# A ten-phase network on one core: the S5 tables are prepared beside another stage, the modulation's matrix is read in three parts

## The chip, the cores and the metric

The kernel runs on one core of a Trainium2 chip. The metric is device time in microseconds, the median of runs. The engines are TensorE (PE, with its weight loads as PEld), VectorE (DVE), ScalarE (ACT), GpSimd (POOL) and SyncE (SP), which only issues transfers here. P is 128, T is 512.

## The reference

Two blocks run one behind the other on an activation of 512 tokens by 1024 channels, all in float32. The first block has a gated delta-net mixer, a convolutional feed-forward network (FFN), a chunked attention and a second FFN. The second block has two layers; each is modulated by six vectors of 1024 that come from the condition `c` by a matrix.

```python
cond = jax.nn.silu(c)
for i in range(DEPTH):
    mod = cond @ ada_w[i] + ada_b[i]                    # 1024 x 6144, for each layer
    sh1, sc1, g1, sh2, sc2, g2 = jnp.split(mod[:, None, :], N_MOD, axis=-1)
    h = _modulate(_rmsnorm(x, norm_mix_g[i]), sh1, sc1)
    y = _s5_mixer(h, ...) if i % 2 == 0 else _ssd_mixer(h, ...)
    x = x + g1 * y
    h = _modulate(_rmsnorm(x, norm_mlp_g[i]), sh2, sc2)
    x = x + g2 * _sq_relu_mlp(h, mlp_w1[i], mlp_w2[i])
```

The S5 mixer is a linear recurrence for 64 groups of 64 complex states. Powers of its transition, and its input and output matrices multiplied by them, depend on parameters alone; the kernel prepares them as tables before the mixer begins.

## The kernel before, in words

The phases run in the order gdn, ffn0, attn, ffn1, s5, mlp0, ssd, mlp1, and a final norm. The activation stays in SBUF as eight tiles `h` of 128 channels by 512 tokens. Every weight matrix is read in chunks of 128 by 1024 float32 (512 KB) in one fixed order, `queue`. `next()` hands out a chunk: ScalarE rounds it to a high part (L305), VectorE subtracts to get the low part (L306), and TensorE takes three matmuls for each pair of parts (L347 to L349), 24 matmuls of 512 columns a chunk. Raw, high and low parts have three buffers each, and the read of a chunk is issued three chunks ahead, from SP's queue.

An FFN has 44 up chunks and 24 down chunks, in the order 20 up, 8 down, 16 up, 8 down, 8 up, 8 down. Behind an up chunk VectorE scales the result (L598), and takes two of three taps of a convolution (L607); once in a pair of chunks it multiplies gate and value (L978) and splits the product (L566). Behind a down chunk it adds to `h` (L577). The MLPs have 32 chunks in and 32 out. Their first four chunks are taken by the stage before as heads.

Work that no phase needs at once runs in the background. `bg` is a list of Python generators, and each call of `next()` advances the first of them by `bgrate` steps. So the background's instructions stand in the program between weight chunks; a scheduler of the framework then orders each engine's instructions by program order and by its own account of when each is ready, and each engine keeps that order on the chip. There are three kinds of background:

- `ada_bg` reads the modulation's matrix in 96 chunks of 512 KB (two buffers, `araw`), multiplies each by its part of the condition and adds it up on VectorE (L1142), in three thirds; each third ends with small matmuls. All three run beside ffn0.
- `shift_bg` sums a shift vector through the head weights of a phase (`s5_in`, the MLPs', the SSD's), 128 columns at a time on VectorE (L1402). The sums for s5 and mlp0 run beside ffn1, those for ssd and mlp1 beside mlp0.
- `s5_prep_bg` prepares the S5 tables beside ffn1, behind the shift sums. Its first five steps compute exponentials, sines and quotients for all groups on VectorE. Then each of eight tiles has five steps: `angles` (VectorE with two sines on ScalarE, on the tiles `exm` and `scm`), `taps` and `b_out` of the tile before, `c_pow` and `b_pow`. The last two are twelve GpSimd instructions of 512 columns a tile and a few small ones. `taps` multiplies their result on TensorE into a bank of PSUM and VectorE writes it to `ks` (L1330), from where eight transfers take it to DRAM; `b_out` transposes `BL` on TensorE (L1356) into two banks. The background's lane has two banks of PSUM, so the second transpose goes to the bank that `taps` used and waits until `ks` has been read from it.

Work tiles of the preparation have one buffer each. `s5_tables` reads the finished tables of a tile back from DRAM, four transfers of 1.8 MB together; the first two tiles' reads are issued with the end of `s5_prep_bg`, the others in the S5 phase.

Of the kernel before, what the change touches and what calls it, by code (L numbers as in the profile page):

```python
# [20 lines left out]
P = 128  # L21
# [199 lines left out]
def r3(ap, n):  # L221
    return ap.rearrange("p (a b) -> p a b", a=n)


class Net:
    def __init__(self, ctx, tc, aps, pcols, out):
# [21 lines left out]
        self.rcol = self.cpool.tile([P, 4], F32, name="rcol")  # L248
# [708 lines left out]
    def ffn(self, l):  # L957
        nc = self.nc
        v, s = nc.vector, nc.scalar
        with ExitStack() as es:  # L960
# [6 lines left out]
            for name, c in self.ffn_seq(l):  # L967
                self.bgrate = 2 if l == 0 and ("down" in name or c >= 36) else 1
# [159 lines left out]
    def ada_bg(self):  # L1128

        nc = self.nc  # L1130
        v = nc.vector
        cond = self.cond
        nc.scalar.activation(cond, self.p("cond"), AF.Silu)
        for q in range(3):
            acc = self.apool.tile([P, 1024], F32, tag="acc", name=self.nm("acc"), bufs=1)
            for k in range(32):
                raw = self.apool.tile([P, 1024], F32, tag="araw", name=self.nm("araw"), bufs=2)
                nc.sync.dma_start(out=raw, in_=self.aps["ada"][q, k])
                if k == 0:
                    v.tensor_scalar(out=acc, in0=raw, scalar1=cond[:, 0:1], scalar2=None, op0=ALU.mult)  # L1140
                else:
                    v.scalar_tensor_tensor(out=acc, in0=raw, scalar=cond[:, k:k + 1], in1=acc,  # L1142
                                           op0=ALU.mult, op1=ALU.add)
                yield
            yield
            ps = self.bank("bg")
            for k in range(8):
                nc.tensor.matmul(ps[:, 4 * k:4 * k + 4], acc[:, k * P:(k + 1) * P], self.p("quarter"),
                                 start=True, stop=True)
            m = slice(32 * q, 32 * q + 32)  # L1150
            v.tensor_tensor(out=r3(self.mods[:, m], 4), in0=ps[:, :32].rearrange("p (k j) -> p j k", k=8),
                            in1=r3(self.p("ada_b")[:, m], 4), op=ALU.add)
        for l in range(2):
            for j in (1, 4):
                v.scalar_tensor_tensor(out=self.gs[l, j], in0=self.mod[l][:, 8 * j:8 * j + 8], scalar=1.0,
                                       in1=self.p(f"nmix{l}" if j == 1 else f"nmlp{l}"), op0=ALU.add, op1=ALU.mult)
# [42 lines left out]
    def s5_prep_bg(self):  # L1199
# [14 lines left out]
        ks = tl(256, "ks")  # L1214
        gp.memset(ks, 0.0)
        zb = [tl(128, nme) for nme in ("zbr", "zbi")]
        for x in zb:
            gp.memset(x, 0.0)
        br, bi = tl(512, "CR"), tl(512, "CI")

        def pair(tag):
            x = self.tpool.tile([P, 1024], F32, tag=tag, name=self.nm("u"))
            return x[:, :T], x[:, T:]
        cr, ci = pair("T")
# [44 lines left out]
        bbr, bbi = pair("B")  # L1269
        t1 = tl(512, "tt")  # L1270
# [22 lines left out]
        def c_pow(t, st):  # L1293
            js, hs = slice(4 * t, 4 * t + 4), slice(64 * t, 64 * t + 64)
            st["C"] = CR, CI = tl(512, "CR"), tl(512, "CI")
# [3 lines left out]
            for o, (x1, l1), (x2, l2), op in ((CR, (cr, lr), (ci, nli), ALU.add),  # L1299
                                              (CI, (cr, nli), (ci, lr), ALU.subtract)):  # L1300
                t1 = tl(512, "tt")
# [3 lines left out]
            st["c0"] = c0 = tl(64, "c0")  # L1305
# [12 lines left out]
        def taps(t, st):  # L1318
            hs = slice(64 * t, 64 * t + 64)
            ps = self.bank("bg")  # L1320
# [15 lines left out]
        def b_pow(t, st):  # L1336
# [5 lines left out]
            for ri in range(2):  # L1342
                o = tl(512, f"BL{ri}")
                t1 = tl(512, "tt")
# [6 lines left out]
        def b_out(t, st):  # L1351
            Bt = tl(1024, "Bt")
# [8 lines left out]
        last = {}  # L1361
        for t in range(8):
            angles(t)
            yield
            for f in (taps, b_out):
                if t:
                    f(t - 1, last)
                    yield
            st = {}
            for f in (c_pow, b_pow):  # L1370
                f(t, st)
                yield
            last = st
# [677 lines left out]
```

## Time and profile before

| | us |
|---|---|
| median of 3 runs | 2775.3 |
| lowest, highest | 2773.09, 2775.48 |
| the profiled execution's time | 2773.28 |
| its span | 2771.5 |
| TensorE busy in it | 2638.3 |
| VectorE busy | 1932.4 |
| ScalarE busy | 1178.4 |
| GpSimd busy | 514.9 |

The span reaches from the first to the last instruction of the program. Busy time of TensorE counts overlapping matmuls once; as matmuls are pipelined, a busy TensorE may still run below its pace, so the spacing of the matmuls' starts and the granted clock are to be read beside it. Idle time of the other engines costs nothing by itself.

### The profile page before, as it was taken

Reading aid. Unit: us, or ns where it says so; the run is one execution under the profiler, and the core shown is the slowest. Engines: PE = TensorE matmul, PEld = TensorE weight load, DVE = VectorE, ACT = ScalarE, POOL = GpSimd, SP = SyncE. Lnnn points to the kernel's source line nnn. Section 1 sums busy time; section 2 is a strip of 40 time slices with the busy share of each in tenths; the row PEclk is TensorE's granted clock in tenths of the full one; section 3 lists DMA queues with packets and bytes.
Section 4 is the critical chain, followed back from the end, with each engine's and each line's share of the span. In section 5 each row is a group of like instructions: output and inputs, shape, how many; then the busy total and the mean of one; then the engine's idle time right before and its main releaser. Section 6 shows DMA issues by size and latency. Waiting matters only on the chain. (4 is left out here: it accounts for less than half of the span.)

```text
span 2771.5 us, 36994 instructions
## 1 busy us (share of the span) xinstructions
PE 2638.3 (95%) x14002; PEld 2121.9 (77%) x14002; DVE 1932.4 (70%) x3332; ACT 1178.4 (43%) x1867; POOL 514.9 (19%) x448
## 2 busy tenths in 40 slices
PE   8899999999999999979998999999999898999998
PEld 6677778888786868767877778888767787778886
DVE  7878889797938689998577565444677767844343
ACT  7555454242437554234264352332554433533232
POOL 0211010000112210446642110000224333300001
PEclk9999999999999999989999999999999999999999
DMA  5323247676733335354449434333333332232322
GB/s 180 121 81 83 75 137 235 214 239 203 232 114 94 109 109 162 99 156 133 145 143 268 130 118 127 98 99 92 93 118 101 114 114 80 71 96 93 99 96 72
DMA packets 172706, 356.34 MB, mean 129 GB/s; under 512 B 44048, under 2 KB 81648, under 8 KB 171504
## 3 DMA queue, kind: packets, MB, share of 16 engines
q1 hardware_dynamic: 163056, 349.78, 40.3%
q10 hardware_dynamic: 9472, 4.20, 0.5%
q8 instruction: 110, 1.80, 0.3%
q14 instruction: 68, 0.56, 0.1%
HBM read 324.00 MB, written 25.72 MB: 126 GB/s over the span
## 5 line engine op out<-in xcount | busy, mean ns | idle before, releaser
L305 ACT CAST hi<-raw 128x1024 fp32r<-128x1024 f32 (+1 forms) x416 | 432.4, 1041 | 863.3 <-PE mm L348 750.2
L347 PE MATMUL mm<-xh,hi 128*128 128x512 f32 x1824 | 739.6, 406 | 23.7 <-ACT hi L305 10.5
L349 PE MATMUL mm<-xh,lo 128*128 128x512 f32 x1824 | 727.2, 399 | 1.1 <-DVE lo L306 1.1
L348 PE MATMUL mm<-xl,hi 128*128 128x512 f32 x1824 | 724.1, 397 | 0.8 <-DVE xl L441 0.8
L306 DVE TENSOR_TENSOR lo<-raw,hi 128x1024 fp32r<-128x1024 f32 (+1 forms) x416 | 529.8, 1274 | 250.8 <-ACT hi L305 243.4
L347 PEld LDWEIGHTS mm<-xh,hi 128*128 128x128 f32 x1824 | 348.5, 191 | 103.3 <-ACT hi L305 14.6
L349 PEld LDWEIGHTS mm<-xh,lo 128*128 128x128 f32 x1824 | 347.2, 190 | 81.1 <-DVE lo L306 3.4
L348 PEld LDWEIGHTS mm<-xl,hi 128*128 128x128 f32 x1824 | 348.2, 191 | 76.8 <-issue 3.2
L347 PE MATMUL mm<-ah,hi 128*128 128x512 f32 x864 | 339.9, 394 | 0.9 <-ACT hi L305 0.7
L349 PE MATMUL mm<-ah,lo 128*128 128x512 f32 x864 | 338.5, 392 | 1.9 <-DVE lo L306 1.9
L348 PE MATMUL mm<-al,hi 128*128 128x512 f32 x864 | 338.3, 392 | 0.0
L481 POOL TENSOR_TENSOR nsq<-nsq,nsq 128x512 f32<-128x512 f32 x54 | 92.6, 1722 | 1161.7 <-ACT nsq L479 764.7
L607 DVE SCALAR_TENSOR_TENSOR cv<-cvr,par,cv 128x511 f32<-128x511 f32 (+2 forms) x248 | 204.8, 826 | 1.5 <-ACT cv L603 0.4
L349 PEld LDWEIGHTS mm<-ah,lo 128*128 128x128 f32 x864 | 163.3, 189 | 37.8 <-DVE lo L306 3.6
L347 PEld LDWEIGHTS mm<-ah,hi 128*128 128x128 f32 x864 | 163.5, 189 | 37.3 <-ACT hi L305 2.5
L348 PEld LDWEIGHTS mm<-al,hi 128*128 128x128 f32 x864 | 163.4, 189 | 34.3 <-DVE al L566 0.4
L579 DVE SCALAR_TENSOR_TENSOR h<-mm,mods,h 128x512 f32<-128x512 f32 x64 | 48.1, 751 | 195.6 <-PE mm L349 195.6
L1142 DVE SCALAR_TENSOR_TENSOR acc<-araw,condt,acc 128x1024 f32<-128x1024 f32 x93 | 121.5, 1307 | 10.1 <-DMA araw<-ada 9.9
L577 DVE TENSOR_TENSOR h<-mm,h 128x512 f32<-128x512 f32 x112 | 76.4, 685 | 65.9 <-PE mm L349 65.5
L347 PE MATMUL mm<-soh,hi 128*128 128x512 f32 x256 | 101.0, 398 | 2.3 <-ACT soh L565 2.3
L348 PE MATMUL mm<-sol,hi 128*128 128x512 f32 x256 | 100.5, 393 | 0.3 <-DVE sol L566 0.3
L349 PE MATMUL mm<-soh,lo 128*128 128x512 f32 x256 | 100.2, 392 | 0.5 <-DVE lo L306 0.5
(530 smaller groups left out, 3946.7 us busy)
## 6 DMA issues: line engine op xcount, KB each, us to landing
raw<-mlp SPq DMA_DIRECT2D x128, 512.0 KB, 3.4
araw<-ada SPq DMA_DIRECT2D x96, 512.0 KB, 4.4
raw<-f_up SPq DMA_DIRECT2D x88, 512.0 KB, 3.9
raw<-m_in SPq DMA_DIRECT2D x40, 512.0 KB, 3.5
raw<-a_in SPq DMA_DIRECT2D x32, 512.0 KB, 4.0
raw<-f_down SPq DMA_DIRECT2D x32, 512.0 KB, 3.9
raw<-b_kv SPq DMA_DIRECT2D x16, 512.0 KB, 3.6
raw<-s_glu SPq DMA_DIRECT2D x16, 512.0 KB, 4.0
```

The source lines that it names most:

```text
L305: self.nc.scalar.copy(hi[:, :sz], raw[:, :sz])
L306: self.nc.vector.tensor_tensor(out=lo[:, :sz], in0=raw[:, :sz], in1=hi[:, :sz].bitcast(F32), op=ALU.subtract)
L347: self.nc.tensor.matmul(ps, a, xh, start=(start and k == 0), stop=False)
L348: self.nc.tensor.matmul(ps, a, xl, start=False, stop=False)
L349: self.nc.tensor.matmul(ps, b, xh, start=False, stop=(stop and k == n - 1))
L481: p.eng.tensor_tensor(out=sq, in0=p.acc[i][-1], in1=sq, op=ALU.add)
L577: nc.vector.tensor_tensor(out=self.h[ot], in0=ps, in1=self.h[ot], op=ALU.add)
L579: nc.vector.scalar_tensor_tensor(out=self.h[ot], in0=ps, scalar=g[:, ot:ot + 1], in1=self.h[ot], op0=ALU.mult, op1=ALU.add)
L607: nc.vector.scalar_tensor_tensor(out=t[:, d:], in0=ps[:, :T - d], scalar=taps[n - 1 - d], in1=t[:, d:], op0=ALU.mult, op1=ALU.add)
L1142: v.scalar_tensor_tensor(out=acc, in0=raw, scalar=cond[:, k:k + 1], in1=acc, op0=ALU.mult, op1=ALU.add)
```

## The change

Four things are moved or widened.

- `s5_prep_bg` runs beside ffn0, alone in the background there, at one step a chunk. Its work tiles `ks`, `zbr`, `zbi`, `CR`, `CI`, `c0`, `tt`, `BL0`, `BL1` and `Bt` get two buffers; the inputs and `bbr`, `bbi` get tiles of their own. Within a tile's turn the order becomes `angles`, `c_pow`, `b_pow`, then `taps` and `b_out` of the tile before.
- `ada_bg` takes a number and reads one third. Beside ffn1 run, in this order, the reads of the first two tiles' tables (`tables_bg`), the first third, the shift sums for s5, the second third, and the shift sums for mlp0. Beside mlp0 run the sums for ssd, the last third, and the sums for mlp1.
- `bgrate` is 2 in the down chunks of ffn1, and 1 elsewhere in both FFNs. Nothing sets it back behind ffn1, so it is 2 beside mlp0 too. Before, it was 2 in ffn0's down chunks and last 8 up chunks, and 1 beside mlp0.
- `rcol` takes 32 columns and uses 4.

The diff, cut to its lines; of `ada_bg` the lines that only change their indentation are left out:

```diff
@@ -245,7 +245,7 @@
-        self.rcol = self.cpool.tile([P, 4], F32, name="rcol")
+        self.rcol = self.cpool.tile([P, 32], F32, name="rcol")[:, :4]
@@ -965,7 +965,7 @@
-                self.bgrate = 2 if l == 0 and ("down" in name or c >= 36) else 1
+                self.bgrate = 2 if l == 1 and "down" in name else 1
@@ -1125,35 +1125,33 @@
-    def ada_bg(self):
+    def ada_bg(self, q):
...
-        for q in range(3):
-            acc = self.apool.tile([P, 1024], F32, tag="acc", name=self.nm("acc"), bufs=1)
-            for k in range(32):
...
+        acc = self.apool.tile([P, 1024], F32, tag="acc", name=self.nm("acc"), bufs=1)
+        for k in range(32):
...
-        for l in range(2):
-            for j in (1, 4):
...
+        for l, j in ([(0, 1)], [(0, 4), (1, 1)], [(1, 4)])[q]:
...
@@ -1211,17 +1209,11 @@
-        ks = tl(256, "ks")
-        gp.memset(ks, 0.0)
-        zb = [tl(128, nme) for nme in ("zbr", "zbi")]
-        for x in zb:
+        kss = [tl(256, f"ks{i}") for i in range(2)]
+        zbs = [[tl(128, f"{nme}{i}") for nme in ("zbr", "zbi")] for i in range(2)]
+        for x in kss + zbs[0] + zbs[1]:
-        br, bi = tl(512, "CR"), tl(512, "CI")
-
-        def pair(tag):
-            x = self.tpool.tile([P, 1024], F32, tag=tag, name=self.nm("u"))
-            return x[:, :T], x[:, T:]
-        cr, ci = pair("T")
+        br, bi, cr, ci = [tl(512, nme) for nme in ("br", "bi", "cr", "ci")]
@@ -1266,8 +1258,8 @@
-        bbr, bbi = pair("B")
-        t1 = tl(512, "tt")
+        bbr, bbi = tl(512, "bbr"), tl(512, "bbi")
+        t1 = tl(512, "tt", 2)
@@ -1292,17 +1284,18 @@
-            st["C"] = CR, CI = tl(512, "CR"), tl(512, "CI")
+            st["C"] = CR, CI = tl(512, "CR", 2), tl(512, "CI", 2)
+            zb = zbs[t % 2]
-                t1 = tl(512, "tt")
+                t1 = tl(512, "tt", 2)
-            st["c0"] = c0 = tl(64, "c0")
+            st["c0"] = c0 = tl(64, "c0", 2)
@@ -1317,7 +1310,7 @@
-            ps = self.bank("bg")
+            ps, ks, zb = self.bank("bg"), kss[t % 2], zbs[t % 2]
@@ -1340,8 +1333,8 @@
-                o = tl(512, f"BL{ri}")
-                t1 = tl(512, "tt")
+                o = tl(512, f"BL{ri}", 2)
+                t1 = tl(512, "tt", 2)
@@ -1349,7 +1342,7 @@
-            Bt = tl(1024, "Bt")
+            Bt = tl(1024, "Bt", 2)
@@ -1358,23 +1351,21 @@
-        last = {}
-        for t in range(8):
-            angles(t)
+        sts = [{} for _ in range(9)]
+        for t in range(9):
+            if t < 8:
+                for f in (lambda t, st: angles(t), c_pow, b_pow):
+                    f(t, sts[t])
+                    yield
+            if t:
+                for f in (taps, b_out):
+                    f(t - 1, sts[t - 1])
+                    yield
+
+    def tables_bg(self):
+        for t in range(2):
+            self.s5_tables(t)
-            for f in (taps, b_out):
-                if t:
-                    f(t - 1, last)
-                    yield
-            st = {}
-            for f in (c_pow, b_pow):
-                f(t, st)
-                yield
-            last = st
-        for t, f in enumerate((taps, b_out)):
-            yield
-            f(7, last)
-            self.s5_tables(t)
@@ -2008,25 +1999,22 @@
-            n.bg.append(n.ada_bg())
+            n.bg.append(n.s5_prep_bg())
-                tags = (("CR", "CI"), ("BL0", "BL1"))
-                n.bg.append(n.shift_bg("s5", 0, 0, [("s5_in", c) for c in range(8)], tags))
-                late = ("ssd", "mlp1") if "mlp0" in second else ()
-                n.bg += [heads(ph, 0 if ph == "mlp0" else 1, tags) for ph in second if ph != "s5" and ph not in late]
-                n.bg.append(n.s5_prep_bg())
+                n.bg += [n.tables_bg(), n.ada_bg(0), n.shift_bg("s5", 0, 0, [("s5_in", c) for c in range(8)]),
+                         n.ada_bg(1), heads("mlp0", 0)]
-                n.bg += [heads(ph, 1) for ph in second if ph in late]
+                n.bg += [heads("ssd", 1), n.ada_bg(2), heads("mlp1", 1)]
```

## Rows read from the trace of the kernel before

**Rows 1.** The page's first line.

```profile
span 2771.5 us, 36994 instructions
```

**Rows 2.** Timeline of SP's queue: start us, us, the transfer issued.

```profile
330.87 0.48 SPq L295 DMA_DIRECT2D raw<-f_up  x1
...
735.68 0.33 SPq L295 DMA_DIRECT2D raw<-b_q  x1
...
973.78 0.33 SPq L295 DMA_DIRECT2D raw<-f_up  x1
...
1415.21 0.33 SPq L295 DMA_DIRECT2D raw<-s_in  x1
```

**Rows 3.** Stretches: from:to, us, busy PE PEld DVE ACT POOL, PEclk, DMA share, GB/s.

```profile
383.00:720.00 337.00, 336.77 (x1490) 276.61 (x1489) 291.63 (x341) 124.10 (x152) 0.00 (x0) 1.00 0.71 224
...
720.00:762.00 42.00, 37.01 (x157) 27.13 (x156) 40.11 (x40) 21.83 (x29) 9.31 (x6) 1.00 0.72 231
...
1104.00:1143.00 39.00, 39.00 (x174) 32.13 (x173) 38.02 (x95) 15.82 (x20) 0.00 (x0) 1.00 0.30 95
1143.00:1195.00 52.00, 37.82 (x175) 29.94 (x174) 50.07 (x70) 7.55 (x13) 42.75 (x40) 0.80 0.38 111
1195.00:1245.00 50.00, 44.17 (x212) 35.34 (x211) 44.31 (x70) 18.48 (x29) 18.93 (x17) 0.93 0.56 173
...
1700.00:1940.00 240.00, 240.00 (x1057) 197.74 (x1056) 99.77 (x114) 72.02 (x90) 0.00 (x0) 1.00 0.31 95
```

**Rows 4.** Waits of PE, 1104 to 1420: us in total, times, longest us.

```profile
PE bg L1356 <- DVE ks L1330: 13.9, 3, 11.0
PE bg L1356 <- POOL BL L1346: 5.8, 1, 5.8
PE bg L1328 <- POOL CI L1304: 3.2, 1, 3.2
```

**Rows 5.** Timeline of PE in the second FFN: start us, us, instruction.

```profile
1149.90 0.39 PE L347 MATMUL mm<-ah,hi 128*128 128x512 f32 x1
1150.13 0.39 PE L348 MATMUL mm<-al,hi 128*128 128x512 f32 x1
...
1168.56 0.63 PE L348 MATMUL mm<-al,hi 128*128 128x512 f32 x1
1168.99 0.63 PE L349 MATMUL mm<-ah,lo 128*128 128x512 f32 x1
```

**Rows 6.** Timeline of DVE in the same stretch, two instructions of one size.

```profile
1158.45 0.29 DVE L1164 TENSOR_SCALAR scm<-exm 128x256 f32<-128x256 f32 x1
...
1167.50 1.25 DVE L1174 TENSOR_SCALAR scm<-exm 128x256 f32<-128x256 f32 x1
```

**Rows 7.** Stretches, instructions on `exm` alone: DVE busy, PEclk, DMA share, GB/s.

```profile
1143.00:1195.00 52.00, 35.88 (x40) 0.80 0.38 111
...
1143.00:1245.00 102.00, 54.52 (x76) 0.87 0.47 142
1204.00:1212.00 8.00, 3.88 (x11) 1.00 0.93 305
```

**Rows 8.** Groups of DVE, 383 to 720: busy us, mean ns | idle before.

```profile
L1142 DVE SCALAR_TENSOR_TENSOR acc<-araw,condt,acc 128x1024 f32<-128x1024 f32 x81 | 103.7, 1280 | 8.6 <-DMA araw<-ada 8.4
L306 DVE TENSOR_TENSOR lo<-raw,hi 128x1024 fp32r<-128x1024 f32 (+1 forms) x59 | 71.1, 1205 | 2.1 <-ACT hi L305 2.0
L607 DVE SCALAR_TENSOR_TENSOR cv<-cvr,par,cv 128x511 f32<-128x511 f32 x88 | 65.6, 745 | 0.2 <-ACT cv L605 0.2
L598 DVE TENSOR_TENSOR cvr<-mm,rb 128x512 f32<-128x512 f32 x44 | 30.1, 685 | 3.7 <-DMA araw<-ada 2.8 <-PE mm L349 0.8
L566 DVE TENSOR_TENSOR al<-cv,ah 128x512 fp32r<-128x512 f32 x22 | 15.1, 685 | 0.0
...
L577 DVE TENSOR_TENSOR h<-mm,h 128x512 f32<-128x512 f32 x16 | 11.0, 690 | 28.4 <-PE mm L349 28.4
```

**Rows 9.** Groups of POOL, 1140 to 1420, one of the table instructions.

```profile
L1347 POOL TENSOR_TENSOR tt<-u,rvi 128x512 f32<-128x512 f32 x16 | 24.1, 1505 | 1.3
```

More of the change, by code (lines that the diff above doesn't have):

```diff
@@ L1132, in ada_bg @@
         cond = self.cond
-        nc.scalar.activation(cond, self.p("cond"), AF.Silu)
-        for q in range(3):
-            acc = self.apool.tile([P, 1024], F32, tag="acc", name=self.nm("acc"), bufs=1)
-            for k in range(32):
[L1137 to L1143, printed above, removed]
-                yield
-            yield
-            ps = self.bank("bg")
[L1147 to L1152, printed above, removed]
@@ L1153, in ada_bg @@
-        for l in range(2):
-            for j in (1, 4):
-                v.scalar_tensor_tensor(out=self.gs[l, j], in0=self.mod[l][:, 8 * j:8 * j + 8], scalar=1.0,
-                                       in1=self.p(f"nmix{l}" if j == 1 else f"nmlp{l}"), op0=ALU.add, op1=ALU.mult)
+        if q == 0:
+            nc.scalar.activation(cond, self.p("cond"), AF.Silu)
+        acc = self.apool.tile([P, 1024], F32, tag="acc", name=self.nm("acc"), bufs=1)
+        for k in range(32):
+            raw = self.apool.tile([P, 1024], F32, tag="araw", name=self.nm("araw"), bufs=2)
+            nc.sync.dma_start(out=raw, in_=self.aps["ada"][q, k])
+            if k == 0:
+                v.tensor_scalar(out=acc, in0=raw, scalar1=cond[:, 0:1], scalar2=None, op0=ALU.mult)
+            else:
+                v.scalar_tensor_tensor(out=acc, in0=raw, scalar=cond[:, k:k + 1], in1=acc, op0=ALU.mult, op1=ALU.add)
+            yield
@@ new lines, in ada_bg @@
+        yield
+        ps = self.bank("bg")
+        for k in range(8):
+            nc.tensor.matmul(ps[:, 4 * k:4 * k + 4], acc[:, k * P:(k + 1) * P], self.p("quarter"),
+                             start=True, stop=True)
+        m = slice(32 * q, 32 * q + 32)
+        v.tensor_tensor(out=r3(self.mods[:, m], 4), in0=ps[:, :32].rearrange("p (k j) -> p j k", k=8),
+                        in1=r3(self.p("ada_b")[:, m], 4), op=ALU.add)
+        for l, j in ([(0, 1)], [(0, 4), (1, 1)], [(1, 4)])[q]:
+            v.scalar_tensor_tensor(out=self.gs[l, j], in0=self.mod[l][:, 8 * j:8 * j + 8], scalar=1.0,
+                                   in1=self.p(f"nmix{l}" if j == 1 else f"nmlp{l}"), op0=ALU.add, op1=ALU.mult)
@@ L1319, in taps @@
             hs = slice(64 * t, 64 * t + 64)
-            ps = self.bank("bg")
+            ps, ks, zb = self.bank("bg"), kss[t % 2], zbs[t % 2]
             js = [slice(32 * j, 32 * j + 32) for j in range(4)]
@@ L1359, in b_out @@
             nc.sync.dma_start(out=self.s5B[t], in_=Bt)
-        last = {}
-        for t in range(8):
-            angles(t)
-            yield
-            for f in (taps, b_out):
-                if t:
-                    f(t - 1, last)
-                    yield
-            st = {}
-            for f in (c_pow, b_pow):
-                f(t, st)
-                yield
-            last = st
-        for t, f in enumerate((taps, b_out)):
-            yield
-            f(7, last)
-            self.s5_tables(t)
+        sts = [{} for _ in range(9)]
[7 more added lines that the diff above has]
+                    f(t - 1, sts[t - 1])
+                    yield
+    def tables_bg(self):
+        for t in range(2):
+            self.s5_tables(t)
+            yield
     def shift_bg(self, key, l, sh, chunks, tags=(("ra0", "rb0"), ("ra1", "rb1"))):
```

## The prediction

> **What bounds the kernel now.** I read the page first [rows 1]: the profiled execution has a span of 2771.5 us and a time of 2773.3 us, so 1.8 us lie around the span; the median of the three runs shown, 2775.3, is 2.0 above it, and all sums below are made against 2773.3. A difference of 0.2%, 5.5 us, is about what a measurement of this kernel can tell from no change.
>
> TensorE is the bound, at a fixed pace: in an undisturbed stretch a matmul of 512 columns starts 0.23 us after the one before [rows 5], so a weight chunk of 24 matmuls takes 5.45 us. The question is where the pace is lost. The issue times of the weights tell it at once [rows 2]. From the first chunk of the first FFN to the first chunk behind it pass 735.7 - 330.9 = 404.8 us; the same steps of the second FFN take 1415.2 - 973.8 = 441.4 us. The weights have one size, so the second FFN loses 36.6 us more than the first.
>
> The table by stretches [rows 3] shows where. In the first FFN, where the modulation's matrix is read, TensorE is busy 336.8 of 337 us with VectorE at 291.6: a nearly full VectorE that costs nothing. In the second FFN nothing is lost until 1143 either. Then GpSimd starts on the S5 tables (42.8 us busy of 52), and TensorE is busy only 37.8 of 52 and 44.2 of 50 us, 20 us lost, at a mean granted clock of 0.80 and 0.93. The list of TensorE's waits for 1104 to 1420 [rows 4] has no weight in it: all three lines are table matmuls in TensorE's own queue, 13.9 us for `ks` on VectorE, 9.0 us for the products `CI` and `BL` on GpSimd, 22.9 us together. The rest of the 36.6 is mostly the clock: after a stall matmuls are spaced 0.43 us [rows 5], the 1.2 GHz level in place of 2.4, for some eleven matmuls.
>
> So the loss sits in the table work, with two causes. GpSimd is late for its products, and VectorE is late because its small table instructions stretch while GpSimd works: a TENSOR_SCALAR of 256 columns takes 0.29 us, or 1.25 us when GpSimd runs [rows 6]. By tile name [rows 7], the eleven instructions that touch `exm` in one tile take 3.9 us undisturbed, 54.5 / 76 x 11 = 7.9 us over 1143 to 1245, and 35.9 / 40 x 11 = 9.9 us in the densest 52 us.
>
> **The change part by part.** *The second FFN loses its tables.* That removes the 36.6 us. In their place come two thirds of the modulation, at one step a chunk in up projections and two in down projections. An up chunk costs VectorE 1.21 + 0.69 + 2 x 0.75 + 0.69 (the two instructions that come once a pair, taken from L566) = 4.1 us, a down chunk 1.21 + 0.69 = 1.9 us, a modulation step 1.28 us [rows 8]. So an up takes 5.4 and a down 4.5 of 5.45 us. This is the mixture that the first FFN carries now at no loss; cover: the matmuls. Without it each step would cost its 1.28 us. The head sums for S5 stay. I take 0 us here.
>
> *The first FFN gets the tables.* They issue from its first chunk, one step a chunk: five steps of preparation, then five a tile, 45 steps, so they are over in the second down group.
> GpSimd: twelve instructions of some 1.5 us a tile [rows 9], 18 us of the 27 us that five chunks last. With two buffers each, and `taps` and `b_out` behind the next tile's `c_pow` and `b_pow`, TensorE asks for a product two steps or more later than before, and the 9.0 us of waits for GpSimd go.
> VectorE keeps the same instructions, in a worse place. Before, preparation and the first tiles fell mostly into down chunks, with 3.5 us spare each; now they fall into up chunks with 1.4 spare. The preparation: VectorE was busy 38.0 us in 1104 to 1143 [rows 3]; seven down chunks of 1.9 leave 24.7, with the last few head sums still among it, so I take 23 us. Over the first 20 up chunks it has 20 x 4.06 = 81 us of main work, 23 of preparation and four tiles of angles at 7.9 each, 32: 136 us, against 20 x 5.45 = 109 of TensorE. That is 27 us late, which appears as waits for `ks` or for the weights' low parts; the eight down chunks behind leave room, so nothing more piles up. Bounds: with angles at 3.9 the same sum is 11 late, and 0 if the preparation finds gaps before the first chunk; with 9.9 it is 35. I take 27, by the mean of the whole overlap, which is the nearest thing to the new mixture.
>
> Is the stretching a lock or only sharing? In [rows 6] the slow instruction takes 1.25 us for 0.29 of work, about one GpSimd instruction more. The Trainium skill, "SBUF — State Buffer", section "Who interferes with whom", says that VectorE's two-port modes and GpSimd hold one port pair exclusively for a whole instruction. By that alone every angle instruction would take about 1.25 us; the time this would give is the last rival's. The trace agrees for single instructions; over the whole overlap the mean of 0.72 us does not.
>
> *The first FFN loses the modulation.* It lost nothing there, so nothing is won, except at its end: the last third runs into the attention, where TensorE is busy 37.0 of 42 us [rows 3]. Some of that is the next stage's own preparation. I take -2 us (0 to -5).
>
> *The tables of tiles 0 and 1* (3.7 MB) are read in the first two steps of the second FFN, on SP ahead of its weights. The fastest transfer rate seen is 305 GB/s [rows 7], so 12 us; two or three weight chunks, 11 to 16 us, lie ready or on their way. I take +2 (0 to +8).
>
> *The first MLP* gets the last third. The rate stays at 2 from the second FFN's last down chunk, so both head sums double in pace too. VectorE has 99.8 of 240 us to do there, 2.3 a chunk [rows 3]; two steps bring 2.6, together 4.9 of 5.45. The transfers are three chunks of 0.52 MB in 5.45 us, 289 GB/s, close to 305. I take +2 (0 to +8).
>
> *Two small edits.* The wider `rcol` shifts addresses; the page shows no cost tied to one, so 0. New buffers for `br`, `cr`, `bbr` and the rest only take memory, 0.
>
> Sum: -36.6 + 27 - 2 + 2 + 2 = -7.6; 2773.3 - 7.6 = 2765.7, taken as 2766. Bounds: -36.6 + 0 - 5 = -42 and -36.6 + 50 + 16 = +29.
>
> **The rivals.**
> *The tables hide* (as the modulation did). For it: VectorE at 87% costs nothing in [rows 3], and the buffers take away both GpSimd waits. Against: the loss came with GpSimd active. Lateness 0 to 11: -36.6 + 5 - 2 + 4 = -30, 2744 us (2736 to 2751).
> *The stall only moves.* At 9.9 us a tile, which the densest stretch had [rows 7], it is 35 us late, and -36.6 + 35 + 2 = +0.4: 2774 us (2769 to 2778). Two buffers speak for it: GpSimd can run two tiles without a pause.
> *Slower: the full alternation.* Each of a tile's eleven angle instructions waits out one of GpSimd's: 11 x 1.25 = 13.8 us a tile, 81 + 23 + 55 = 159 against 109, 50 late: -36.6 + 50 + 2 = +15, 2789 us (2780 to 2800). The exclusive port of the Trainium skill would give this same time. The case decides from about 10.3 us a tile on (36.6 - 2 = 34.6 late). The row of 1.25 speaks for it, the mean of 7.9 against.
>
> **How the numbers follow.** The forecast 0.38 (2757 to 2769), tables hidden 0.18, the stall moves 0.22, slower 0.22. The forecast's own span lies mostly below 2767.8, the point where 0.2% begins: 0.32 of it counts as faster and 0.06 as same. Faster 0.32 + 0.18 = 0.50; same 0.06 + 0.20 = 0.26; slower 0.22 + 0.02 = 0.24. The range 2742 to 2788 leaves out about a third of the hidden case and half of the slower one, under 2 in 10.
>
> **What would show it.** The steps of the second FFN (first chunk to S5's first chunk) should fall from 441 to about 405 us, with no `ks`, `CI` or `BL` among TensorE's waits and GpSimd idle. The first FFN should rise from 405 to about 430, with VectorE full in its first 20 chunks, `exm` instructions near 0.7 us, and waits for `ks` or the low parts but none for GpSimd. The MLP should keep TensorE at 240 of 240. I am wrong if the first FFN stays near 405 (hidden), if it passes 440 (the stall moved or grew), if waits for `BL` or `CI` return there, or if the second FFN or the MLP waits for weights.

## The result, and the profile after

The changed kernel takes 2823.6 us (median of 4 runs, 2821.7 to 2828.0) against 2775.3 before: a ratio of 1.0176, 95% interval 1.0163 to 1.0188. It is 48 us slower; the forecast was 2766, its range ended at 2788. The profiled execution took 2828.0 us.

The first line of the page after, and the issue times of the first weights of each stage in SP's timeline, which answer to [rows 1, 2]:

```profile
span 2826.2 us, 36947 instructions
```
```profile
340.27 0.33 SPq L295 DMA_DIRECT2D raw<-f_up  x1
...
804.78 0.33 SPq L295 DMA_DIRECT2D raw<-b_q  x1
...
1047.16 0.33 SPq L295 DMA_DIRECT2D raw<-f_up  x1
...
1453.86 0.33 SPq L295 DMA_DIRECT2D raw<-s_in  x1
...
1626.64 0.33 SPq L295 DMA_DIRECT2D raw<-mlp  x1
...
2000.33 0.33 SPq L295 DMA_DIRECT2D raw<-m_in  x1
```

The first MLP's two lines in the kernel before:

```profile
1593.20 0.33 SPq L295 DMA_DIRECT2D raw<-mlp  x1
...
1949.80 0.33 SPq L295 DMA_DIRECT2D raw<-m_in  x1
```

The second FFN fell from 441.4 to 406.7 us, as forecast. The first rose from 404.8 to 464.5 and the first MLP from 356.6 to 373.7. Where in the first FFN shows in its stretches (columns as in [rows 3]); the last two lines are from the second FFN and from the MLP:

```profile
340.00:426.00 86.00, 81.71 (x468) 62.76 (x468) 72.28 (x170) 42.71 (x74) 13.22 (x18) 0.98 0.26 81
426.00:583.00 157.00, 116.37 (x543) 90.56 (x542) 151.59 (x203) 47.71 (x71) 105.16 (x91) 0.86 0.34 101
583.00:805.00 222.00, 222.00 (x1116) 178.39 (x1116) 143.18 (x160) 80.11 (x104) 59.92 (x50) 1.00 0.42 126
1100.00:1440.00 340.00, 340.00 (x1497) 276.96 (x1496) 293.02 (x412) 123.86 (x152) 0.00 (x0) 1.00 0.68 216
1700.00:1940.00 240.00, 234.00 (x1008) 190.47 (x1007) 142.38 (x183) 70.06 (x90) 0.00 (x0) 0.97 0.51 165
```

The loss lies in 426 to 583: VectorE is busy 151.6 of 157 us, GpSimd 105.2, TensorE only 116.4 at a granted clock of 0.86. Behind 583, when the angles are done, TensorE is never idle and its clock is 1.00, though GpSimd still works 59.9 us there. TensorE's waits in the first FFN (340 to 805) and in the MLP:

```profile
PE bg L1349 <- DVE ks L1323: 16.3, 2, 9.8
PE mm L349 <- DVE lo L306: 15.8, 4, 10.6
PE bg L1349 <- POOL zbi L1304: 8.6, 1, 8.6
...
PE bg L1147 <- DVE acc L1142: 6.0, 1, 6.0
```

`ks` and the weights' low parts are both VectorE's. What VectorE did in 426 to 583, by groups, is the table to read against [rows 8]; below it is the same table for 1143 to 1245 of the kernel before, the stretch of [rows 7]:

```profile
L306 DVE TENSOR_TENSOR lo<-raw,hi 128x1024 fp32r<-128x1024 f32 x18 | 27.9, 1552 | 0.8 <-ACT hi L305 0.8
...
L607 DVE SCALAR_TENSOR_TENSOR cv<-cvr,par,cv 128x510 f32<-128x510 f32 x14 | 16.7, 1190 | 0.0
L607 DVE SCALAR_TENSOR_TENSOR cv<-cvr,par,cv 128x511 f32<-128x511 f32 x14 | 14.7, 1049 | 0.0
L598 DVE TENSOR_TENSOR cvr<-mm,rb 128x512 f32<-128x512 f32 x14 | 9.5, 682 | 0.0
L566 DVE TENSOR_TENSOR al<-cv,ah 128x512 fp32r<-128x512 f32 x8 | 8.4, 1051 | 0.7 <-ACT ah L565 0.7
...
L978 DVE TENSOR_TENSOR cv<-cv,cv 128x512 f32<-128x512 f32 x7 | 6.8, 975 | 0.0
```
```profile
L306 DVE TENSOR_TENSOR lo<-raw,hi 128x1024 fp32r<-128x1024 f32 x12 | 16.8, 1398 | 0.0
...
L607 DVE SCALAR_TENSOR_TENSOR cv<-cvr,par,cv 128x510 f32<-128x510 f32 x5 | 4.7, 948 | 0.0
...
L598 DVE TENSOR_TENSOR cvr<-mm,rb 128x512 f32<-128x512 f32 x5 | 3.4, 683 | 0.0
```

Not only the table instructions are stretched, the FFN's own are too. An up chunk costs VectorE 1.55 + 0.68 + 1.05 + 1.19 + (1.05 + 0.98) / 2 = 5.5 us where the prediction had 4.1, more than the 5.45 us of its matmuls before any table work. Three forms of it stood in the trace before at 1.40, 0.95 and 0.68. The form that takes one operand from PSUM (L598) is not stretched.

These means are mixtures of two durations. The timelines of GpSimd and VectorE in the same stretch of the changed kernel, columns as in [rows 5]:

```profile
473.37 1.25 POOL L1339 TENSOR_TENSOR BL<-bbi,mg 128x512 f32<-128x512 f32 x1
474.58 1.73 POOL L1341 TENSOR_TENSOR BL<-BL,tt 128x512 f32<-128x512 f32 x1
476.27 1.12 POOL L1340 TENSOR_TENSOR tt<-bbr,rvi 128x512 f32<-128x512 f32 x1
...
478.87 1.34 POOL L1341 TENSOR_TENSOR BL<-BL,tt 128x512 f32<-128x512 f32 x1
```
```profile
473.61 1.55 DVE L607 SCALAR_TENSOR_TENSOR cv<-cvr,par,cv 128x510 f32<-128x510 f32 x1
475.09 1.38 DVE L1169 TENSOR_SCALAR scm<-exm 128x256 f32<-128x256 f32 x1
476.38 1.56 DVE L978 TENSOR_TENSOR cv<-cv,cv 128x512 f32<-128x512 f32 x1
...
478.98 0.68 DVE L598 TENSOR_TENSOR cvr<-mm,rb 128x512 f32<-128x512 f32 x1
```

The two engines take turns. GpSimd's instruction of 473.37 ends at 474.62, and VectorE's L607, issued meanwhile, ends 0.54 us behind it, at 475.16; GpSimd's next one ends 1.15 us behind that, at 476.31; VectorE's L1169 (0.28 us undisturbed) 0.16 us behind that; and so on. Of these, L598 alone runs its 0.68 us through a GpSimd instruction without waiting. Of the 80 instructions on `exm` in 426 to 583, 45 took 0.28 to 0.48 us, as undisturbed, and 35 took 0.56 to 1.51. Of the 18 of L306, 11 took 1.21 to 1.25 and 7 took 1.52 to 2.28; of the 28 of L607, 16 took up to 0.77 and 12 took 1.54 to 1.78. Counted over both timelines, 69 VectorE instructions without an operand in PSUM started with more than 0.35 us of a GpSimd instruction left, and 65 of them waited until it ended; the 4 with an operand in PSUM that started so did not wait. The same holds in the kernel before: of the 76 instructions of [rows 7], 44 took 0.28 to 0.46 us and 32 took 0.89 to 1.41.

### The profile page after: what moved, and what is told of

It is laid out like the page before. It is cut to its first block, busy times and chain, and to the rows that moved or that the text cites. A ratio compares the mean times of both kernels' runs of the same rounds, so it can differ in the third digit from the quotient of the medians.

```text
span 2826.2 us, 36947 instructions
## 1 busy us (share of the span) xinstructions
PE 2668.6 (94%) x14002; PEld 2131.6 (75%) x14002; DVE 1947.5 (69%) x3332; ACT 1178.8 (42%) x1867; POOL 517.9 (18%) x451
## 5 line engine op out<-in xcount | busy, mean ns | idle before, releaser
L349 PE MATMUL mm<-xh,lo 128*128 128x512 f32 x1824 | 735.1, 403 | 16.6 <-DVE lo L306 16.5
L348 PE MATMUL mm<-xl,hi 128*128 128x512 f32 x1824 | 735.1, 403 | 0.0
L306 DVE TENSOR_TENSOR lo<-raw,hi 128x1024 fp32r<-128x1024 f32 (+1 forms) x416 | 528.9, 1272 | 245.6 <-ACT hi L305 239.1
L347 PEld LDWEIGHTS mm<-xh,hi 128*128 128x128 f32 x1824 | 349.3, 191 | 114.1 <-ACT hi L305 14.5
L607 DVE SCALAR_TENSOR_TENSOR cv<-cvr,par,cv 128x511 f32<-128x511 f32 (+2 forms) x248 | 205.7, 830 | 2.4 <-ACT cv L605 0.9
L577 DVE TENSOR_TENSOR h<-mm,h 128x512 f32<-128x512 f32 x112 | 76.6, 685 | 78.5 <-PE mm L349 78.1
L598 DVE TENSOR_TENSOR cvr<-mm,rb 128x512 f32<-128x512 f32 x112 | 76.7, 685 | 49.3 <-PE mm L349 45.6
```

Of the source, the lines that this page charges most:

```text
L306: self.nc.vector.tensor_tensor(out=lo[:, :sz], in0=raw[:, :sz], in1=hi[:, :sz].bitcast(F32), op=ALU.subtract)
L347: self.nc.tensor.matmul(ps, a, xh, start=(start and k == 0), stop=False)
L348: self.nc.tensor.matmul(ps, a, xl, start=False, stop=False)
L349: self.nc.tensor.matmul(ps, b, xh, start=False, stop=(stop and k == n - 1))
L577: nc.vector.tensor_tensor(out=self.h[ot], in0=ps, in1=self.h[ot], op=ALU.add)
L598: nc.vector.tensor_tensor(out=pr, in0=ps, in1=r, op=ALU.mult)
```

## The experiments

Stage lengths are differences of issue times, taken as above, in the one profiled execution of each run. Each ratio is against runs of the kernel before on the same chip, with its 95% interval.

| run | median us | ratio | first FFN | second FFN | first MLP |
|---|---|---|---|---|---|
| before | 2775.3 | | 404.8 | 441.4 | 356.6 |
| after | 2823.6 | 1.0176 (1.0163 to 1.0188) | 464.5 | 406.7 | 373.7 |
| e1_rcol4 | 2808.1 | 1.0110 (1.0095 to 1.0126) | 460.1 | 402.3 | 371.1 |
| e2_mlp_rate1 | 2815.0 | 1.0139 (1.0117 to 1.0160) | 464.5 | 406.6 | 364.1 |
| e3_no_angles | 2797.5 | 1.0072 (1.0057 to 1.0088) | 442.3 | 406.6 | 369.8 |
| e3b_no_angles | 2792.9 | 1.0064 (1.0045 to 1.0084) | 436.7 | 408.3 | 373.7 |
| e4_quarter_products | 2789.6 | 1.0046 (1.0028 to 1.0064) | 433.0 | 408.3 | 369.9 |
| e5_one_buffer | 2807.2 | 1.0109 (1.0087 to 1.0131) | 448.2 | 406.6 | 371.6 |
| e18_three_undone | 2778.5 | 1.0007 (0.9996 to 1.0018) | 446.1 | 403.9 | 360.2 |
| e7_angles_apart | 2761.6 | 0.9950 (0.9934 to 0.9967) | 425.6 | 403.9 | 361.9 |
| e9_prep_spread | 2760.9 | 0.9946 (0.9931 to 0.9962) | 426.4 | 402.2 | 361.5 |
| e12_spread_one_buffer | 2750.8 | 0.9910 (0.9894 to 0.9925) | 416.1 | 402.1 | 358.6 |
| e17_spread_shift64 | 2746.9 | 0.9900 (0.9883 to 0.9916) | 417.2 | 401.8 | 357.6 |

**The angles left out.** The first try:

```diff
-            v.tensor_tensor(out=r3(x, 4), in0=bc(t8[:, 4 * t:4 * t + 4], 64), ...)
-            self.sincos(pool, x, 256, cs[:, :256], cs[:, 256:])
+            for hf in (cs[:, :256], cs[:, 256:]):
+                s.copy(r3(hf, 4), self.p("cc").unsqueeze(1).to_broadcast([P, 4, 64]))
```

> The changed kernel without the angles' work: each tile's eleven VectorE instructions and two sines are left out, two plain ScalarE copies fill the tile that is stored, so the first stored table is not the reference's. GpSimd's products stay. Theory (VectorE and GpSimd slow each other, and the up chunks have too little spare VectorE time for both the angles and the stretched main work): the first FFN falls from 464.5 to 410 to 420 us, the time to about 2774. Rival one, GpSimd's products alone stretch VectorE's main work enough: it keeps 435 or more, the time 2795 or more. Rival two, the order in which the table matmuls stand in TensorE's queue behind GpSimd's products sets the loss: it stays over 450, the time over 2808.

The first FFN took 442.3 us, between the theory and rival one. But the edit had brought its own wait: ScalarE's copies stood behind the store of the one `cs` tile (the three longest waits of ScalarE, 440 to 547; the second is the one meant):

```profile
ACT ah L565 <- DVE cv L978: 24.2, 6, 5.8
ACT cs L1281 <- DMA s5R<-cs: 17.4, 3, 15.1
ACT cv L975 <- DVE cv L607: 15.4, 5, 4.2
```

So the run decides little, and was made again without that wait:

```diff
+        cs = tl(512, "cs")
+        gp.memset(cs, 0.0)
         def angles(t):
-            x, cs = tl(NK, "exm")[:, :256], tl(512, "cs")
-            v.tensor_tensor(...)
-            self.sincos(...)
```

> The changed kernel with the angles left out whole: one cleared tile is stored for each of the eight tiles, so that neither VectorE nor ScalarE has work or a wait there (in the run before, ScalarE's copies waited 17.4 us for those stores). GpSimd's products stay. If the 65 us of angle instructions and the stretching of the main VectorE instructions (5.5 us an up chunk in place of 4.1) together made the loss, the main work alone fits the matmuls again nearly: the first FFN takes 425 to 435 us (24 us for the preparation, which stays), the time about 2785 to 2792. If the stretching alone is enough, it stays at 440 us or more and the time at 2797.

436.7 us, 28 less than after, just above the first theory's span. Taking the angles out wins about half of the loss. Without them GpSimd was busy 88.1 of the 103 us from 440 to 543, and an up chunk's main work was stretched further (L306 1.58 us, L607 1.44 and 1.35), so both halves of the theory hold.

**GpSimd's products cut to a quarter.**

```diff
-                gp.tensor_tensor(out=b4(o), in0=bc(r3(x1[:, hs], 4), 8), in1=lk(l1), op=ALU.mult)
+                q = slice(0, 1)
+                gp.tensor_tensor(out=b4(o)[:, q], in0=bc(r3(x1[:, hs], 4), 8)[:, q], in1=lk(l1)[:, q], op=ALU.mult)
...
```

> The changed kernel with GpSimd's twelve products of a tile cut to a quarter of their columns (128 of 512, the rest of the tables stay zero), in buffers cleared once; VectorE's work stays whole. Theory: the angles go back toward 0.35 us an instruction, the main instructions to their old durations, and the first FFN falls from 464.5 to 405 to 420 us (by the sum of the prediction with 3.9 us of angles a tile, 11 us late, 416): time about 2770 to 2780. Rival: VectorE's table work is too much for the up chunks by itself, whatever GpSimd does: the stage keeps 440 or more, the time 2800 or more.

433.0 us: 31.5 less, not the 405 to 420 expected and not the rival's 440. VectorE's groups of 426 to 543 are nearly back at their old durations, main and table instructions both:

```profile
L306 DVE TENSOR_TENSOR lo<-raw,hi 128x1024 fp32r<-128x1024 f32 x18 | 23.6, 1310 | 0.8 <-ACT hi L305 0.8
L607 DVE SCALAR_TENSOR_TENSOR cv<-cvr,par,cv 128x510 f32<-128x510 f32 x14 | 11.4, 814 | 0.0
L1168 DVE SCALAR_TENSOR_TENSOR exm<-scm,exm 128x256 f32<-128x256 f32 x24 | 11.3, 471 | 0.2
```

L1168 took 0.78 us after. GpSimd's products are thus the cause of the stretching. Of the 28 us that are left, 24 arise in the first 12 chunks: the 13th weight is issued 112.0 us behind the first, against 87.8 before and 112.4 after (106.0 in e3b). The preparation, five steps in the first five chunks, stands there, and neither edit touches it. No run takes it out alone; where it was spread over the up chunks (e7 below), the 13th weight was issued at 87.1, and the loss came behind it. The two edits won 27.8 and 31.5 us, together more than the 35 us of the loss that arise behind the 13th weight: the angles and the products cost most of it where they meet, and taking away either one wins it.

**One buffer each.** The changed placement with the buffers and step order of before:

```diff
-            st["C"] = CR, CI = tl(512, "CR", 2), tl(512, "CI", 2)
+            st["C"] = CR, CI = tl(512, "CR"), tl(512, "CI")
...
-                for f in (lambda t, st: angles(t), c_pow, b_pow):
+                angles(t)
...
+            for f in (taps, b_out):
...
+            for f in (c_pow, b_pow):
```

> The changed kernel's placement with the preparation's buffers and order of steps of the kernel before (one buffer each, `taps` and `b_out` of the tile before ahead of `c_pow` and `b_pow`), rates and all else as changed. Theory: VectorE's load in the first FFN is the same with one buffer, so the stage still takes 450 to 470 us and the time is within 10 us of 2823. Rival one, two buffers hurt, because GpSimd then works without a pause beside VectorE: 430 to 440 us, time about 2797. Rival two, they help as the prediction had it, because TensorE no longer waits for GpSimd: without them 475 us or more, time over 2833.

448.2 us and 2807.2: 16 faster than with two. The theory's 450 was too high and rival one's direction was right: two buffers with their order of steps cost; the run does not tell buffers and order apart. With one, GpSimd is busy 88.6 of the 140 us from 426 to 566 (0.63) in place of 0.67, and the instructions on `exm` take 0.67 us in place of 0.73 (48.18 / 72 and 58.70 / 80), because 27 of 72 were held in place of 35 of 80.

**The rate beside the first MLP.**

```diff
             with tc.tile_pool(name="bgp3", bufs=1) as n.apool:
+                n.bgrate = 1
```

> The changed kernel with the background's rate set back to 1 ahead of the first MLP. Theory: the MLP lost 17.1 us (356.6 to 373.7) because two steps a chunk ask for two chunks of the modulation's matrix beside one of weights, which comes too late for the small matmuls that stand in TensorE's queue. At one step a chunk the stage goes to 357 to 360 us and the time to about 2808. Rival: the third itself costs the time there, by VectorE or by the bytes, at any rate: the stage stays over 368 and the time at 2818 or more.

The stage took 364.1 us, between the two expected spans and 9.6 less than after, with `acc` gone from TensorE's waits; the time fell by 8.6 to 2815.0. So the rate is about half of the 17.1 us; 7.5 remain at rate 1. At rate 2 the reads had been late (waits of VectorE, 1690 to 1820; then two stretches of the stage after):

```profile
DVE acc L1142 <- DMA araw<-ada: 17.9, 18, 1.8
```
```profile
1760.00:1800.00 40.00, 34.00 (x146) 27.73 (x145) 28.94 (x33) 10.41 (x15) 0.00 (x0) 0.89 0.73 234
1800.00:1820.00 20.00, 20.00 (x81) 15.87 (x80) 15.64 (x44) 6.50 (x9) 0.00 (x0) 0.87 0.37 113
```

TensorE waits 6.0 us for `acc` with the third's small matmuls at the head of its queue, and the clock is low for some 20 us behind it.

**The wider `rcol`**, undone in the changed kernel, and done alone in the kernel before:

```diff
-        self.rcol = self.cpool.tile([P, 32], F32, name="rcol")[:, :4]
+        self.rcol = self.cpool.tile([P, 4], F32, name="rcol")
```

> The changed kernel with `rcol` back at 4 columns, nothing else. In the changed kernel's profile the gated delta-net, which runs no background, takes 340.3 us in place of 330.9, though its instructions are the same. If the shifted addresses cost these 9.4 us, this run's delta-net is back near 331 and the time falls to about 2814. If it is one execution's variation, the time stays at 2823 within 3 us, whatever this profile shows of that stage. The first FFN stays at 460 to 465 us by either.

> The kernel before with `rcol` at 32 columns, nothing else. Narrowing it in the changed kernel took 15 us off, spread over many stages, and the matmuls' starts stood 229 in place of 231.5 ns apart with the same granted clock. If the addresses do that, this kernel is 10 to 18 us slower than the one before, with each FFN and the second MLP 3 to 5 us longer. If the 15 us were the difference between two chips or two runs, it takes the same time within 4 us.

Undone it gave 15.5 us back (2808.1), more than the 9.4 looked for, with the delta-net at 335.7 us; done alone it took the kernel before from 2774.7 to 2790.9, ratio 1.0058 (1.0035 to 1.0081). It is a cost of its own, not in the delta-net alone (that stage took 330 to 337 us in the runs with 4 columns and 332 to 343 in those with 32). Part of the matmuls start farther apart: in 200 us of the second MLP, with clock 1.00 and TensorE never idle, the kernel before starts 879 matmuls, with the wide `rcol` 868.

Six more runs of the kernel before asked what of the address decides, each with only the width changed (`[P, 8]`, `[P, 36]`, `[P, 16]`, `[P, 24]`, `[P, 72]`), the last with a pad of 24 columns opened behind the weights' pool. The framework lays tiles out in steps of 32 bytes, so 8 columns moved nothing (the expectation's 16 bytes were wrong) and that run is the kernel before once more.

> The kernel before with `rcol` at 8 columns, which moves what lies behind it by 16 bytes a partition, where 32 columns moved it by 112 and cost 16 us. If the slower spacing comes from where the addresses stand within 32 bytes (112 is 16 modulo 32), this costs the same 12 to 18 us; if it comes from where they stand within 64 or 128 bytes, it may cost nothing.

> The kernel before with `rcol` at 36 columns, a shift of 128 bytes a partition. If the position within 128 bytes or a smaller power of two decides, this takes the time of the kernel before within 4 us; if any shift costs, or what meets in a larger stride, 10 us or more.

> The kernel before with `rcol` at 16 columns: tiles are laid out in steps of 32 bytes, so what lies behind moves by 32 bytes a partition. If any shift of the weights against the activation's high and low tiles costs, the time is some 16 us over the kernel before; if 32 bytes are small enough, within 4 us.

> The kernel before with `rcol` at 24 columns, a shift of 64 bytes. If the place within 64 bytes decides, this is within 4 us of the kernel before and a shift of 32 is not; but 128 bytes cost 16 us, which speaks for 16 us here too.

> The kernel before with `rcol` at 72 columns, a shift of 256 bytes. If the place within 256 bytes decides, within 4 us of the kernel before; if a larger stride, or any shift, 16 us slower.

> The kernel before with a tile of 24 columns (96 bytes) between the weights' pool and all pools behind it, `rcol` as before: the weights stay where they were, all stage tiles move by 96 bytes. If the place of the weights against the activation's high and low tiles is the cause, the time is that of the kernel before within 4 us; if the stage tiles are, 16 us slower.

| moved, bytes | ratio | matmuls in 2500 to 2700 |
|---|---|---|
| 0 (8 columns) | 0.9999 (0.9989 to 1.0010) | 879 |
| 32 | 1.0047 (1.0029 to 1.0066) | 868 |
| 64 | 0.9983 (0.9970 to 0.9995) | 884 |
| 96 (32 columns) | 1.0058 (1.0035 to 1.0081) | 868 |
| 128 | 1.0063 (1.0046 to 1.0080) | 868 |
| 256 | 1.0003 (0.9993 to 1.0013) | 878 |
| 96, behind the weights only | 1.0052 (1.0032 to 1.0072) | 868 |

The last line seems to rule out the place of the weights against the activation, and its expectation reads it so. But the 200 us mix two kinds of matmuls: those of the MLP's first matrix take the activation from `xh` and `xl`, which lie ahead of `rcol`; those of the second take it from `ah` and `al`, which are stage tiles behind the pad. Stretches of one kind each, first `xh` and `xl`, then `ah` and `al`, in the kernel before, with 32 columns, and with the pad:

```profile
2594.00:2669.00 75.00, 75.00 (x329) 61.56 (x328) 34.18 (x41) 28.46 (x40) 0.00 (x0) 1.00 0.30 94
2671.00:2756.00 85.00, 85.00 (x377) 70.35 (x376) 29.71 (x31) 19.23 (x23) 9.39 (x6) 1.00 0.21 69
```
```profile
2605.00:2680.00 75.00, 75.00 (x323) 60.40 (x322) 33.49 (x40) 28.05 (x39) 0.00 (x0) 1.00 0.28 91
2684.00:2769.00 85.00, 85.00 (x376) 70.41 (x375) 29.68 (x31) 18.90 (x22) 9.39 (x6) 1.00 0.21 69
```
```profile
2610.00:2685.00 75.00, 75.00 (x329) 61.54 (x328) 34.19 (x41) 28.52 (x40) 0.00 (x0) 1.00 0.29 94
2687.00:2772.00 85.00, 85.00 (x366) 68.39 (x365) 29.72 (x31) 19.21 (x23) 8.08 (x5) 1.00 0.21 69
```

The wide `rcol` moves the weights against `xh` and `xl`, and only those matmuls slow down (323 for 329 in 75 us); `ah` and `al` move with the weights, and theirs keep their pace (376 for 377 in 85 us). The pad moves `ah` and `al` against the weights, and only those slow down (366). So the place of the weights against the activation that a matmul reads sets its pace; the last line's 868 is the other kind of matmul slowed. Which property of the distance decides is open: no single power of two fits (128 costs, 256 doesn't).

**Do the causes add up?** `rcol`, rate and buffers undone together:

> The changed kernel with `rcol` at 4, rate 1 beside the first MLP, and the kernel before's buffers and order of steps; only the placement is left, with the angles in each tile's turn. If the costs found one at a time add up, 2823.6 - 15.5 - 8.6 - 16.4 = 2783 us within 5, with the first FFN at 440 to 446 us. If GpSimd's density and the rest overlap in what they cost, 2788 or more.

2778.5 us, 45 less than after, where 40.5 were expected from the single runs, and a first FFN of 446.1. They add up within the 5 us allowed. The placement by itself is worth nothing: 1.0007 (0.9996 to 1.0018), 37.5 won in the second FFN and 41.3 lost in the first.

**The angles apart.** With `rcol` at 4 and rate 1, the eight angles stand ahead of the tiles' products, and fewer steps go into up chunks:

```diff
+                if l == 0 and "up" in name and c < 20:
+                    self.bgrate = c % 2
+                elif l == 0 and "up" in name:
+                    self.bgrate = c % 4 != 3
...
+        for t in range(8):
+            angles(t)
+            yield
         for t in range(9):
-                for f in (lambda t, st: angles(t), c_pow, b_pow):
+            for f in (c_pow, b_pow):
...
```

The runs after it have `c % 4 == 3` in place of `c % 2`, and the last two of them e5's buffers and order too; the very last has `rcol` at 24 columns.

> A version that follows from the theory: `rcol` at 4, rate 1 beside the first MLP, and in the first FFN the eight angles stand ahead of all of GpSimd's products of the tiles (five steps of preparation, eight angles, then products, `taps` and `b_out` in turn), at one step in two of the first 20 up chunks, three in four of the later ones, one in each down chunk. Theory: the angles then run undisturbed at about 4 us a tile, and GpSimd's products stand only beside main work: the first FFN takes 415 to 435 us, the time is 2757 to 2778. Rival: GpSimd's stretching of the main work or the preparation alone keeps the stage over 440 us: 2783 or more.

2761.6 us, first FFN 425.6: as the theory had it, and the first version faster than the kernel before. The angles are not all undisturbed: the 71 instructions on `exm` from 417 to 532 take 0.50 us each, 11 of them held. Its remaining loss sits in chunks 12 to 16, which take 49.8 us (21.9 before).

> The version with the angles apart, which took 2761.6 us and lost 28 of its 21 extra us in the first FFN within chunks 12 to 16, where preparation, first angles and GpSimd's first products met; here the background moves only one step in four of the first 20 up chunks, so that the five steps of preparation fill them and the angles belong to the eight down chunks. Theory (VectorE's spare time has to lie where the work lies): the first FFN falls from 425.6 to 410 to 420 us, the time to about 2748 to 2757. Rival: each engine's order is set by when an instruction is ready and not by its step, so the work stands where it stood and the stage stays at 424 us or more, the time at 2760 or more.

A miss: 426.4 us, the rival's case (by "28 of its 21 extra" the 28 us lost up to chunk 16 are meant, of which some are won back later). Chunks 12 to 16 improved to 34.7 us, 16 to 20 went from 21.9 to 37.2: the loss moved by four chunks. The rival's mechanism shows in GpSimd's queue: it is busy 44.6 of the 60 us from 424 to 484 with preparation and first products, though the products' steps stand behind the first 28 chunks, and the 29th weight is issued only at 539.

> The same as the run before it, with one buffer for each work tile of the tables and `taps` and `b_out` of the tile before ahead of `c_pow` and `b_pow`. In the changed placement one buffer was 16 us faster, because GpSimd worked less densely beside VectorE. If density is what counts, this is as fast as two buffers or up to 8 us faster. Rival: with the angles out of the way TensorE again waits for `ks` and for GpSimd's products, as in the second FFN of the kernel before: 8 us slower or more.

2750.8 us, first FFN 416.1, a little better than the expected 8 us. With one buffer, GpSimd runs less far ahead into the stretch where preparation and angles stand: it is busy 28.8 of the 60 us from 424 to 484. The run's stretches, and TensorE's waits in that FFN:

```profile
424.00:484.00 60.00, 54.66 (x223) 43.61 (x222) 59.37 (x104) 21.96 (x30) 28.83 (x23) 0.94 0.29 88
484.00:528.00 44.00, 44.00 (x195) 36.30 (x194) 42.23 (x88) 19.51 (x29) 0.00 (x0) 1.00 0.39 126
528.00:618.00 90.00, 90.00 (x457) 73.01 (x456) 68.36 (x74) 33.08 (x43) 42.33 (x34) 1.00 0.43 132
```
```profile
PE mm L349 <- DVE lo L306: 3.4, 2, 2.4
PE mm L347 <- DVE h L577: 2.7, 3, 2.1
```

From 484 to 528 stand angles without products: GpSimd is idle, the 49 instructions on `exm` take 17.25 us, 0.35 each, and nothing is lost with VectorE busy 42.2 of 44 us. From 528 on stand products beside main work: VectorE is busy 76% of the time, and nothing is lost. Products beside a full VectorE are what costs.

> The fastest version so far (angles apart, preparation spread, one buffer, 2750.8 us) with `rcol` at 24 columns, the layout in which the kernel before had its matmuls 227.0 in place of 228.4 ns apart. If the layout carries over, some 10 thousand matmuls of 1.4 ns less, about 6 us by the kernel before's own difference: 2742 to 2748. If not, 2751 or more.

2746.9 us; 884 matmuls in 2500 to 2700 against 879, so the pace carried over, but the two intervals overlap and the 4 us are not shown.

## Why the prediction was wrong, step by step

- **What bounds the kernel, and the second FFN: right.** It lost its 36.6 us: 402.3 us with the narrow `rcol` (39.1 won), 406.7 as changed. TensorE is busy 340 of 340 there with two thirds of the modulation beside it.
- **The first FFN's tables, +27: this step failed.** With the narrow `rcol` it measured +55.3. Its price of angles came out: the ten instructions on `exm` take 58.70 / 80 = 0.73 us each and the one on `scm` alone 0.6, 8.0 us a tile (7.9 predicted). That price is the share of instructions held by GpSimd, 35 of 80 here and 32 of 76 before, and not a duration of its own, so the agreement is in part luck. Three other parts were wrong. First, "20 x 4.06 = 81 us of main work" took the main instructions at the undisturbed prices of [rows 8]; beside GpSimd an up chunk costs 5.5. The prediction stretched the table instructions and not the others, though the stretch of before that it took 7.9 from shows both. Second, "the eight down chunks behind leave room, so nothing more piles up": between 426 and 583, in 18 weight chunks, all eight tiles' angles ran (80 instructions, ten a tile), where the program has one tile's in five steps. The queues are ordered by readiness too, and angles need no product of GpSimd's; [rows 7] had it too, 76 instructions in 102 us. When the 21st weight was issued the stage was 44.9 us behind before's, at the 29th 67. Third, spare time was pooled over 20 chunks, but the preparation stands in the first ones and the stage was 24 us late by the 13th weight; what VectorE has to spare later does not return what TensorE lost.
- **The sum with measured prices.** An estimate for the first 28 chunks: 151 us by the prediction's prices with four tiles, + 21 for the main work (86.7 us in 426 to 583, L577 with it; 18 x 1.21 + 28 x 0.75 + 33 x 0.69 = 65.6 at undisturbed prices), + 32 for four more tiles: 204 against 153 of TensorE, 51 late. The rest of the 67, 16 us, no run tells apart; the low clock (0.86 over 157 us) and the tables' own matmuls on TensorE lie in it.
- **Lock or sharing: answered wrongly.** The prediction had found single instructions held as by a lock, and set that aside because "over the whole overlap the mean of 0.72 us does not" agree. A mean cannot tell: the timelines after the result show instructions either undisturbed or held until GpSimd's instruction ends, main and table instructions alike. L306, L607, L566 and L978, with two SBUF inputs, went from means of 1.21, 0.75, 0.69 and 0.69 to 1.55, 1.05 to 1.19, 1.05 and 0.98; L598, with one operand in PSUM, stayed at 0.68. The prediction weighed one rule of the Trainium skill ("SBUF — State Buffer", section "Who interferes with whom"), the exclusive port in two-port modes. The same section of the Trainium skill says that a VectorE instruction with two SBUF inputs contends with a GpSimd instruction that reads SBUF, and one with at most one SBUF input, outside those modes, does not. The trace agrees with both: the four named were held, and L598's 14 stayed at 0.68 to 0.69 us. L1169, with one input, was held as well; that it runs in a two-port mode no row here shows.
- **"The 9.0 us of waits for GpSimd go": wrong.** 8.6 us are still put down to GpSimd, and the two buffers with their order of steps cost 16 us, with GpSimd working more densely.
- **The end of the first FFN, -2.** From chunk 28 on the stage took 221.8 us in place of 229.5, 7.7 won and not 2. No run says how much of it is the modulation's absence.
- **The first MLP, +2: mis-sized.** +17.1, of it 9.6 by the rate and some 3 by `rcol` (371.1 with it narrow); what is left, 4.5, no run tells apart. Three chunks in 5.45 us, 289 GB/s, was called close to the fastest rate seen; the stretch reached 234, and the wait fell on matmuls in TensorE's own queue, with a low clock behind it.
- **`rcol`, 0: wrong.** 16 us, in the matmuls whose weights moved against their activation. No row of the trace before could show it.
- **The rivals.** The slower one (2789) had the right sign, and its mechanism, an exclusive alternation, is what the timelines show where both engines have work. It had it at all eleven instructions of a tile, 13.8 us, where 35 of 80 were held, and at none of the main ones. The border that it names, 10.3 us a tile, is a slip: 81 + 23 + 4 x 9.9 = 143.6 against 109 is already 34.6 late, so it is 9.9.

Together 55.3 + 14.5 (the MLP with the narrow `rcol`) + 16 - 39.1 = 46.7 of the 48.3 us.

## What to carry to other kernels

When work for a second engine is moved beside a stage, price the stage's own instructions at their durations beside that engine, not only those that move. Look at single rows before reading a mean: the 0.73 us here are 45 instructions at some 0.36 and 35 at some 1.2. Independent background work does not keep to its step: count in the trace how much of it runs at once, and separate in time what slows each other. More buffers can let an engine run denser, which is a loss where its work holds up the one that sets the end.

## What was not expected of the hardware

The width of a small tile set the matmuls' pace: 868 to 884 starts in the same 200 us at granted clock 1.00, by shifts of 32 to 256 bytes that move the weights against the activation that the matmul reads, or this activation against the weights. VectorE and GpSimd hold each other up instruction by instruction, and the slowing goes both ways: in e3_no_angles, the same GpSimd product took 1.52 us beside a busy VectorE (9.2 of 10 us) and 1.06 when VectorE was idle (0.06 of 10):

```profile
450.51 1.52 POOL L1338 TENSOR_TENSOR BL<-bbi,mg 128x512 f32<-128x512 f32 x1
...
466.60 1.06 POOL L1338 TENSOR_TENSOR BL<-bbi,mg 128x512 f32<-128x512 f32 x1
```
